# Reordering matmuls, first loads and one reduction chain in a conformer-plus-attention layer on one core

## The chip, the core and the metric

The kernel runs on one NeuronCore of a Trainium2 chip. The core has a matrix engine (PE, with a weight-load part PEld), a vector engine (DVE), a scalar engine (ACT), a GpSimd engine (POOL), a queue engine (SP), and 16 DMA engines. Each engine works through its own instruction list in order; semaphores connect the lists. The metric is the device time of one execution in microseconds (us), given as the median over runs. The time before the change is 2009.45 us, the median of 3 runs (2008.85 to 2011.46).

## The reference

One layer on 512 tokens of 2048 features, in float32:

```python
xn = rms_norm(x, attn_norm_g);  proj = xn @ w_in            # 2048 -> 5120 columns
u_val, u_gate, q, k, v = split(proj)
y_conv = silu(layer_norm(depthwise_conv31(u_val * sigmoid(u_gate))))
y_na   = neighborhood_attention(q, k, v, rpb)               # 16 heads of 64, window 8 x 16 on a 8 x 64 grid
x = x + concat(rms_norm(y_conv), rms_norm(y_na)) @ w_out    # 2048 -> 2048
xn = rms_norm(x, ffn_norm_g);  up = depthwise_conv3(xn @ w_up)   # 2048 -> 2 * 5632
x = x + (silu(gate) * val) @ w_down                         # 5632 -> 2048
return rms_norm(x, final_norm_g)
```

## The kernel before, in words

**Precision.** Every weight unit of 128 x 1024 floats is loaded by SP into a buffer `raw` (nine of them, `NR`), rounded by ACT into a high part `whi` (L125), and the remainder is taken by DVE into a low part `wlo` (L126). There are four buffers of each part (`NW`). Activations are split in the same way (`xh` and `xl`, `mah` and `mal`). A product is the sum of three matmuls: high by high, high weight by low activation, low weight by high activation. `mm3` (L138, L141, L142) issues the three for one block of 128 rows, one after the other. `weights()` hands out the units in the order of `plan`, and makes each unit three units ahead of its use (`AHEAD`).

**Input projection (up to about 515 us).** `project(n)` makes one tile of 128 output columns by 512 tokens from two units of eight blocks, so 48 matmuls of 512 columns. The first two tiles (`first_glu`) use units loaded by hand in a fixed order (`early`, `piece`, `pin`); `pin` keeps an instruction at its place in the program order on its engine, while the others are placed by a scheduler that goes by priorities. `stats1` is a generator that `tick` advances once after each unit; it loads the untransposed input in eight pieces (`xn`, L305), squares each on ACT with a running sum (L306), and makes from the sums the row factor `rstd1` by `root_steps` (the small DVE steps L224 to L234, then a matmul `st` at L237, and an ACT copy at L239). `gated` multiplies by `rstd1` (L352, L354, L356), and appends the 31 convolution steps of a tile (L363, L367) on DVE. The attention of a head pair runs in steps between the units (`sc`, `trp`, `trv` and `po` matmuls).

**Output projection (to about 708 us).** `out_half` makes 16 tiles of 512 columns from one unit each, once for the convolution half (`ma`) and once for the attention half (`mb`). In the second pass `after(d, ps)` adds the tile to the residual `x2[d]`, adds its square to `acc2` (`sum_sq`, L211 and L212), turns the tile by four PE transposes (`turned`, L594) and writes it to memory, and for each pair of tiles makes the seven operand sums of a Strassen-like scheme: scaled tiles `b` (L611), sums `t` (L616 to L621), and their high and low parts `xc` (`halves`, L586 and L587) into `comb[c]`.

**Up projection (to about 1577 us).** For each of 44 values of `f`, `up` makes seven products in the order `TURN = (3, 2, 4, 5, 1, 0, 6)`. An `xc` tile holds the high part in its first 256 columns and the low part in the other 256, so the high weight takes one matmul of 512 columns and the low weight one of 256 columns (L696): eight of the first, then eight of the second. Product 2 is made by `mm3` with three matmuls of 256 columns for each block. ACT copies and DVE adds combine the products (`copied` L706, `folded` L709 and L710). `stats2` makes `rstd2` from `acc2` during `f = 0`.

**Down projection (to the end).** `product2` makes seven products of 22 units each, into four PSUM banks. For each bank, `feed` issues three matmuls (L821 high by high, L822 with the low weight, L823 with the low activation). The last four units of the last product are done bank by bank.

Of the kernel before, what the change touches and what calls it, by code (L numbers as in the profile page):

```python
# [10 lines left out]
F32 = mybir.dt.float32  # L11
# [5 lines left out]
P = 128  # L17
D = 2048
# [32 lines left out]
NEG = -1.0e30  # L51

TURN = (3, 2, 4, 5, 1, 0, 6)
TURN2 = (3, 0, 4, 1, 2, 6, 5)
Q = D // 2 // S
TAIL = 4
# [16 lines left out]
def layer(ctx: ExitStack, tc: tile.TileContext, xT, xn, w_in, w_out, w_up, w_down, par, tab, g3, out):  # L73
# [28 lines left out]
    def pc(name, i):  # L102
        o = POFF[name] + i
        return prm[:, o:o + 1]
# [30 lines left out]
    def mm3(ps, w, wk, mh, ml, start, stop, more=False):  # L135
        hi, lo = w[:2]
        a = slice(wk * P, (wk + 1) * P)
        i = nc.tensor.matmul(ps, hi[:, a], mh, start=start, stop=False, skip_group_check=more)  # L138
        if tight:
            pin(i)  # L140
        nc.tensor.matmul(ps, hi[:, a], ml, start=False, stop=False, skip_group_check=more)  # L141
        return nc.tensor.matmul(ps, lo[:, a], mh, start=False, stop=stop, skip_group_check=more)  # L142


    steps, asteps = [], []

# [105 lines left out]
    def split_x(k):  # L252
        x1.append(t2("x"))
        i = pin(nc.sync.dma_start(x1[k], xT[k]))
        h, l = t2("xh", F32R), t2("xl", F32R)
        pin(nc.scalar.activation(h, x1[k], AF.Copy, scale=g1[:, k:k + 1]))
        pin(nc.vector.scalar_tensor_tensor(l, x1[k], g1[:, k:k + 1], h.bitcast(F32), op0=ALU.mult, op1=ALU.subtract))
        xs.append((h, l))
        return i
# [26 lines left out]
    for i in range(4):  # L286
# [7 lines left out]
    del plan[4:8]  # L294
# [20 lines left out]
    def project(n):  # L315
        ps = psm.tile([P, S], F32, tag="mm", name="pj")
        for u in range(KD // U):
            w = weights()
            for k in range(U):
                kk = u * U + k  # L320
                m = mm3(ps, w, k, xs[kk][0], xs[kk][1], kk == 0, kk == KD - 1)
            tick(m)
            if weights.at > 6 and weights.at % 2:
                sum_ahead(m)
            while late:
                late.pop()()
        return ps
# [223 lines left out]
    def out_half(m, read):  # L551
        for d in range(KD):
            w = weights()
            ps = psm.tile([P, S], F32, tag="mm", name="po2")
            for k in range(U):
                i = mm3(ps, w, k, m[k][0], m[k][1], k == 0, k == U - 1)
            tick(i)
            if d % 3 == 0:
                sum_ahead(i)
            read(d, ps)  # L560
# [38 lines left out]
    def after(d, ps):  # L599

        t = t2("oa")
        nc.vector.tensor_mul(t, ps, rb[0])
        nc.vector.tensor_add(x2[d], x2[d], t)
        sum_sq(acc2, x2[d], d == 0)
        turned(d)
        if d % 2 == 0:
            return
        b = []
        for i in (d - 1, d):
            t = t2("b")  # L610
            nc.scalar.activation(t, x2[i], AF.Copy, scale=pc("g2", i))  # L611
            b += [t[:, :H], t[:, H:]]
        b11, b12, b21, b22 = b
        t = t2("t")
        t1, t2_ = t[:, :H], t[:, H:]
        nc.vector.tensor_sub(t1, b11, b12)  # L616
        nc.vector.scalar_tensor_tensor(t2_, b22, -1.0, t1, op0=ALU.mult, op1=ALU.subtract)
        t = t2("t")
        t3, t4_ = t[:, :H], t[:, H:]
        nc.vector.tensor_sub(t3, b22, b12)  # L620
# [10 lines left out]

    def stats2():
        rstd2.append((yield from rsqrt_steps(acc2, D, "rstd2")))

    def factors(f, at):

# [48 lines left out]
    def up(f, done):  # L685

        def product(c, ps, more):
            hi, lo = wt = weights()
            if c == 2:
                for k in range(U):  # L690
                    m = comb[c][k]
                    i = mm3(ps[:, :H], wt, k, m[:, :H], m[:, H:], k == 0, k == U - 1)
            else:
                for part, n in ((hi, S), (lo, H)):
                    for k in range(U):
                        i = nc.tensor.matmul(ps[:, :n], part[:, k * P:(k + 1) * P], comb[c][k][:, :n],  # L696
                                             start=part is hi and k == 0 and not more,
                                             stop=part is lo and k == U - 1, skip_group_check=more)
                        if part is hi and k == 0 and tight:
                            pin(i)  # L700
            tick(i)
            done(TURN.index(c), i)

        def copied(to, ps):
            with shifted(-100):
                nc.scalar.activation(to, ps, AF.Copy)  # L706

        def folded(to, ps):
            nc.scalar.activation(to, ps[..., H:], AF.Copy)  # L709
            add(to, to, ps[..., :H])  # L710
# [102 lines left out]

    def product2(c, ps, more):

        def feed(w, h, i, start, stop):
            wh, wl = w
            t, d = divmod(i, Q)
            t, d = slice(t * P, (t + 1) * P), slice(d * S, (d + 1) * S)
            tl = slice(H + t.start, H + t.stop)  # L820
            nc.tensor.matmul(ps[i], h[:, t], wh[:, d], start=start and not more, stop=False, skip_group_check=more)  # L821
            nc.tensor.matmul(ps[i], h[:, t], wl[:, d], start=False, stop=False, skip_group_check=more)  # L822
            return nc.tensor.matmul(ps[i], h[:, tl], wh[:, d], start=False, stop=stop, skip_group_check=more)  # L823

        n = NK - TAIL if c == TURN2[-1] else NK
        for j in range(n):
            w, h = weights()
            for i in range(2 * Q):
                m = feed(w, h, i, j == 0, j == NK - 1)
            tick(m)  # L830
        if n < NK:
            got = [weights() for _ in range(NK - n)]
            assert not steps
            for i in range(2 * Q):
                for j, (w, h) in enumerate(got):
                    feed(w, h, i, False, j == NK - n - 1)
                yield i

    def rest(th, dh):
# [162 lines left out]
```

## Time and profile before

| | us |
|---|---|
| median of 3 runs | 2009.45 |
| the profiled execution, its own time | 2008.65 |
| its span in the trace | 2006.9 |
| PE busy | 1985.5 (99%) |
| DVE busy | 1598.5 (80%) |
| ACT busy | 1095.9 (55%) |

The span reaches from the first to the last instruction. A row of the timeline has the start, the duration, the engine, the line, the operation, the tiles, the shape and a count, and in brackets how long the engine had been idle and what ended it. Matmuls overlap in the pipeline, so the duration of one in the trace is longer than the step from one start to the next; the step is what counts here. In the view by windows each row has a stretch, then each engine's busy time and count, then the granted PE clock, the DMA share and the GB/s.

### The profile page before, as it was taken

The numbers are of one execution on the slowest core, as the hardware profiler recorded it, in microseconds if no ns is written. First come the engines' busy times: TensorE is split into PE (matmuls) and PEld (weight loads), VectorE is DVE, ScalarE is ACT, GpSimd is POOL, SyncE is SP. The second block draws the span as 40 slices with busy tenths as digits, with TensorE's granted clock in tenths as the row PEclk, the third lists the DMA queues.
The fourth block names the chain that finished last, engine by engine and source line by source line (L and its number), as shares of the span: only waits on it lengthen the run. The fifth ranks groups of instructions, "written<-read, shape, count | busy, mean of one in ns | idle before, by whom it ended". The sixth has DMA issues, their size and how long they took to land.

```text
span 2006.9 us, 28334 instructions
## 1 busy us (share of the span) xinstructions
PE 1985.5 (99%) x10525; PEld 1688.0 (84%) x10525; DVE 1598.5 (80%) x2296; ACT 1095.9 (55%) x1728; POOL 225.8 (11%) x310
## 2 busy tenths in 40 slices
PE   9999999999999999999999999999999999999998
PEld 7778888887788889888898988898898888888886
DVE  4994899488556888888888888888888898886765
ACT  6234433447534666566666666566666644554654
POOL 0111111111001111111111111111110400000000
PEclk9999999999999999999999999999999999999999
DMA  9677767766858888989999999999997877666563
GB/s 352 158 197 180 177 172 190 192 182 166 296 147 206 214 213 230 271 237 260 249 260 247 261 252 253 258 250 262 250 246 200 335 254 235 216 217 191 191 213 110
DMA packets 143115, 451.01 MB, mean 225 GB/s; under 512 B 15232, under 2 KB 23936, under 8 KB 141568
## 3 DMA queue, kind: packets, MB, share of 16 engines
q1 hardware_dynamic: 90608, 293.98, 43.0%
q0 software_dynamic: 42624, 148.92, 34.7%
q10 hardware_dynamic: 9744, 6.30, 1.0%
q8 instruction: 82, 1.34, 0.3%
q14 instruction: 57, 0.47, 0.1%
HBM read 430.27 MB, written 111.15 MB: 270 GB/s over the span
## 4 chain that ended last, share of the span: by engine, by line
PE 96%; DVE 2%; ACT 1%; DMA 1%; issue 0%; SPq 0%; DVEq 0%; ACTq 0%
PE pu L696 37%; PE pd L821 7%; PE pd L822 7%; PE pd L823 7%; PE pj L138 7%; PE pj L141 7%; PE pj L142 7%; PE po L138 3%; PE po L141 3%; PE po L142 3%; PE pu L141 2%; PE pu L142 2%; PE pu L138 2%; DVE y L367 1%; PE po L495 1%; PE sc L453 1%
## 5 line engine op out<-in xcount | busy, mean ns | idle before, releaser
L125 ACT ACTIVATE whi<-raw 128x1024 fp32r<-128x1024 f32 x572 | 605.4, 1059 | 709.7 <-PE pj L141 220.4
L126 DVE TENSOR_TENSOR wlo<-raw,whi 128x1024 fp32r<-128x1024 f32 x572 | 698.7, 1222 | 285.2 <-ACT whi L125 261.1
L696 PE MATMUL pu<-xc,whi 128*128 128x512 f32 x2112 | 529.8, 392 | 0.2 <-ACT pu L706 0.2
L696 PEld LDWEIGHTS pu<-xc,whi 128*128 128x128 f32 x2112 | 379.9, 189 | 68.8 <-issue 0.5
L696 PEld LDWEIGHTS pu<-xc,wlo 128*128 128x128 f32 x2112 | 288.1, 190 | 20.5
L696 PE MATMUL pu<-xc,wlo 128*128 128x256 f32 x2112 | 294.5, 282 | 0.0
L142 PE MATMUL pj<-xh,wlo 128*128 128x512 f32 x624 | 244.7, 392 | 7.1 <-DVE wlo L126 7.1
L138 PE MATMUL pj<-xh,whi 128*128 128x512 f32 x624 | 247.5, 399 | 0.0
L141 PE MATMUL pj<-xl,whi 128*128 128x512 f32 x624 | 245.0, 393 | 0.1
L821 PE MATMUL pd<-whi,ho 128*128 128x512 f32 x616 | 239.7, 389 | 0.5 <-DVE vl L710 0.5
L822 PE MATMUL pd<-wlo,ho 128*128 128x512 f32 x616 | 239.8, 389 | 0.0
L823 PE MATMUL pd<-whi,ho 128*128 128x512 f32 x616 | 239.5, 389 | 0.0
L367 DVE SCALAR_TENSOR_TENSOR y<-ch,prm,y 128x509 f32<-128x509 f32 (+14 forms) x240 | 170.0, 740 | 3.2
L142 PEld LDWEIGHTS pj<-xh,wlo 128*128 128x128 f32 x624 | 118.0, 189 | 33.0 <-DVE wlo L126 8.0
L138 PEld LDWEIGHTS pj<-xh,whi 128*128 128x128 f32 x624 | 118.0, 189 | 28.4 <-issue 3.7
L141 PEld LDWEIGHTS pj<-xl,whi 128*128 128x128 f32 x624 | 117.8, 189 | 24.3 <-issue 0.7
L821 PEld LDWEIGHTS pd<-whi,ho 128*128 128x128 f32 x616 | 115.7, 188 | 25.0 <-DVE vl L710 0.9
L823 PEld LDWEIGHTS pd<-whi,ho 128*128 128x128 f32 x616 | 115.7, 188 | 24.1
L822 PEld LDWEIGHTS pd<-wlo,ho 128*128 128x128 f32 x616 | 115.7, 188 | 24.1 <-DVE wlo L126 0.3
L194 POOL DMA_DIRECT2D ws<-in_w_down x88 | 79.4, 902 | 495.8 <-DMA ws<-ws 254.8
L643 POOL DMA_DIRECT2D raw<-in_w_up x88 | 86.1, 979 | 408.2 <-ACT vl L709 133.1
L138 PE MATMUL pu<-xc,whi 128*128 128x256 f32 x352 | 99.8, 284 | 1.4 <-ACT xc L586 1.4
(185 smaller groups left out, 2526.0 us busy)
## 6 DMA issues: line engine op xcount, KB each, us to landing
raw<-in_w_up SPq DMA_DIRECT2D x220, 512.0 KB, 7.2
ws<-in_w_down POOLq DMA_DIRECT2D x132, 512.0 KB, 7.4
raw<-in_w_up POOLq DMA_DIRECT2D x88, 512.0 KB, 8.5
raw<-ws SPq DMA_DIRECT2D x88, 512.0 KB, 3.4
raw<-in_w_in SPq DMA_DIRECT2D x78, 512.0 KB, 4.8
raw<-in_w_down SPq DMA_DIRECT2D x66, 512.0 KB, 4.2
ws<-ws POOLq DMA_DIRECT2D x44, 512.0 KB, 7.5
raw<-in_w_out SPq DMA_DIRECT2D x32, 512.0 KB, 4.9
```

The costliest lines, as they stand in the source:

```text
L125: i = nc.scalar.activation(hi[:, :n], raw[:, :n], AF.Copy)
L126: j = nc.vector.tensor_sub(lo[:, :n], raw[:, :n], hi[:, :n].bitcast(F32))
L138: i = nc.tensor.matmul(ps, hi[:, a], mh, start=start, stop=False, skip_group_check=more)
L141: nc.tensor.matmul(ps, hi[:, a], ml, start=False, stop=False, skip_group_check=more)
L142: return nc.tensor.matmul(ps, lo[:, a], mh, start=False, stop=stop, skip_group_check=more)
L194: nc.gpsimd.dma_start(wsum[c][k], w_down[k, {1: A21, 2: A11, 4: A11, 6: A12}[c]], accum_op=ALU.add, max_dma_last_dim=ROW)
L367: nc.vector.scalar_tensor_tensor(y[:, a:b], h[:, a + j - PAD:b + j - PAD], prm[:, o + j:o + j + 1], y[:, a:b], op0=ALU.mult, op1=ALU.add)
L643: nc.gpsimd.dma_start(a[c], w_up[f, q2], accum_op=ALU.add)
L696: i = nc.tensor.matmul(ps[:, :n], part[:, k * P:(k + 1) * P], comb[c][k][:, :n], start=part is hi and k == 0 and not more, stop=part is lo ...
L821: nc.tensor.matmul(ps[i], h[:, t], wh[:, d], start=start and not more, stop=False, skip_group_check=more)
L822: nc.tensor.matmul(ps[i], h[:, t], wl[:, d], start=False, stop=False, skip_group_check=more)
L823: return nc.tensor.matmul(ps[i], h[:, tl], wh[:, d], start=False, stop=stop, skip_group_check=more)
```

## The change

There are five edits, and the arithmetic is the same sums in another order.

1. Low parts last. A new function `group` replaces `mm3` in `project` and `out_half`: for a unit of eight blocks it issues the sixteen matmuls with the high weight, and then the eight with the low weight. In `product2`, `feed` goes by kind: high by high for all banks, then the low activation, then the low weight. `first_glu` and product 2 of `up` keep `mm3`.
2. First loads. The two units of the third projected tile (`NC_ + 1`) and the eight pieces of `xn` with their squares move from the plan and from `stats1` into the pinned opening, in front of the load of the parameters `prm`. `stats1` is left with waiting three ticks, the reduction and the root.
3. The last pair's sums. In `after`, the scaled tile `b` is made as soon as its `x2[d]` is there, the seven operands of a pair are made and split in the order in which `up` uses them, and `sum_sq` comes behind them. `turned` comes one or two tiles later, and for the last tile after the statistics in `stats2`.
4. Order in `up`. The products in `FIRST = (3, 5, 0)` issue the 512-column matmuls first; the products 4, 1 and 6 issue the 256-column matmuls with the low weight first.
5. For `f = 0` product 3 goes block by block, 512 and 256 columns in turn.

```diff
+FIRST = (3, 5, 0)
...
+    def group(ps, ws, ms, first, last):
+
+        for k, ((hi, _, wk), (mh, ml)) in enumerate(zip(ws, ms)):
+            hi = hi[:, wk * P:(wk + 1) * P]
+            nc.tensor.matmul(ps, hi, mh, start=first and k == 0, stop=False)
+            nc.tensor.matmul(ps, hi, ml, start=False, stop=False)
+        for k, ((_, lo, wk), (mh, _)) in enumerate(zip(ws, ms)):
+            i = nc.tensor.matmul(ps, lo[:, wk * P:(wk + 1) * P], mh, start=False, stop=last and k == len(ws) - 1)
+        return i
...
     for k in range(U, KD):
-        last = split_x(k)
+        split_x(k)
+    squares = sm.tile([P, S // P, 2], F32, tag="ss", name="ss")
+    for u in range(2):
+        raw, i = raw_unit(w_in[NC_ + 1, :, u * U * P:(u + 1) * U * P], U * P)
+        pin(i)
+        for t in range(2 * u, 2 * u + 2):
+            for i in range(2):
+                x = t4([P, D // 2], "xn")
+                pin(nc.sync.dma_start(x, xn[t * P:(t + 1) * P, i * D // 2:(i + 1) * D // 2]))
+                if t == 2 * u and i == 0:
+                    w = parts(raw, U * P)
+                    pin(w[2])
+                    pin(w[3])
+                    early.append(w[:2])
+                pin(nc.scalar.activation(x, x, AF.Square, accum_out=squares[:, t, i:i + 1]))
     last = pin(nc.sync.dma_start(prm, par))
...
     def stats1():
-        part = sm.tile([P, S // P, 2], F32, tag="ss", name="ss")
-        for t in range(S // P):
-            for i in range(2):
-                x = t4([P, D // 2], "xn")
-                nc.sync.dma_start(x, xn[t * P:(t + 1) * P, i * D // 2:(i + 1) * D // 2])
-                nc.scalar.activation(x, x, AF.Square, accum_out=part[:, t, i:i + 1])
-            if t < S // P - 1:
-                yield
+        for _ in range(3):
+            yield
         sums = sm.tile([P, S // P], F32, tag="s1", name="s1")
-        nc.vector.tensor_reduce(sums, part, axis=AX.X, op=ALU.add)
+        nc.vector.tensor_reduce(sums, squares, axis=AX.X, op=ALU.add)
...
-            for k in range(U):
-                kk = u * U + k
-                m = mm3(ps, w, k, xs[kk][0], xs[kk][1], kk == 0, kk == KD - 1)
+            m = group(ps, [(*w, k) for k in range(U)], xs[u * U:(u + 1) * U], u == 0, u == KD // U - 1)
...
-        sum_sq(acc2, x2[d], d == 0)
-        turned(d)
+        t = t2("b")
+        nc.scalar.activation(t, x2[d], AF.Copy, scale=pc("g2", d))
+        bs[d % 2] = t[:, :H], t[:, H:]
         if d % 2 == 0:
             return
...
+        halves(b11, 3)
+        nc.vector.tensor_sub(t3, b22, b12)
+        halves(t3, 2)
         nc.vector.tensor_sub(t1, b11, b12)
         nc.vector.scalar_tensor_tensor(t2_, b22, -1.0, t1, op0=ALU.mult, op1=ALU.subtract)
+        halves(t2_, 4)
+        halves(b21, 5)
+        halves(t1, 1)
         nc.vector.scalar_tensor_tensor(t4_, t2_, -1.0, b21, op0=ALU.mult, op1=ALU.subtract)
-        for c in TURN:
-            halves((t4_, t1, t3, b11, t2_, b21, b22)[c], c)
+        halves(t4_, 0)
+        halves(b22, 6)
+        for i in (d - 1, d):
+            sum_sq(acc2, x2[i], i == 0)
+        for i in (d - 2, d - 1):
+            if i >= 0:
+                turned(i)
...
         rstd2.append((yield from rsqrt_steps(acc2, D, "rstd2")))
+        turned(KD - 1)
...
-                for part, n in ((hi, S), (lo, H)):
-                    for k in range(U):
+                turns = [(part, n, k) for part, n in ((lo, H), (hi, S))[::-1 if c in FIRST else 1]
+                         for k in range(U)]
+                if f == 0 and c == 3:
+                    turns.sort(key=lambda a: a[2])
...
+        def feed(got, banks, start, stop):
+
+            for kind in range(3):
+                for i in banks:
+                    t, d = divmod(i, Q)
+                    d = slice(d * S, (d + 1) * S)
+                    for j, ((wh, wl), h) in enumerate(got):
+                        o = H if kind == 1 else 0
+                        w = wl if kind == 2 else wh
+                        m = nc.tensor.matmul(ps[i], h[:, o + t * P:o + (t + 1) * P], w[:, d],
...
```

More of the change, by code (lines that the diff above doesn't have):

```diff
@@ L283, in layer @@
     for k in range(U, KD):
-        last = split_x(k)
+        split_x(k)
[13 more added lines that the diff above has]
+                pin(nc.scalar.activation(x, x, AF.Square, accum_out=squares[:, t, i:i + 1]))
     last = pin(nc.sync.dma_start(prm, par))
-    for i in range(4):
+    for i in range(len(early)):
         plan.append(lambda i=i: early[i])
@@ L293, in layer @@
                 plan.append(lambda n=n, u=u: unit(w_in[n, :, u * U * P:(u + 1) * U * P], U * P))
-    del plan[4:8]
+    del plan[6:12]
     for half in range(2):
@@ L554, in out_half @@
             ps = psm.tile([P, S], F32, tag="mm", name="po2")
-            for k in range(U):
-                i = mm3(ps, w, k, m[k][0], m[k][1], k == 0, k == U - 1)
+            i = group(ps, [(*w, k) for k in range(U)], m, True, True)
             tick(i)
@@ L693, in product @@
             else:
-                for part, n in ((hi, S), (lo, H)):
[L695 to L700, printed above, removed]
+                turns = [(part, n, k) for part, n in ((lo, H), (hi, S))[::-1 if c in FIRST else 1]
+                         for k in range(U)]
+                if f == 0 and c == 3:
+                    turns.sort(key=lambda a: a[2])
+                for j, (part, n, k) in enumerate(turns):
+                    i = nc.tensor.matmul(ps[:, :n], part[:, k * P:(k + 1) * P], comb[c][k][:, :n],
+                                         start=j == 0 and not more, stop=j == 2 * U - 1, skip_group_check=more)
+                    if j == 0 and tight:
+                        pin(i)
             tick(i)
@@ L814, in product2 @@
     def product2(c, ps, more):
[L816 to L823, printed above, removed]
+        def feed(got, banks, start, stop):
[7 more added lines that the diff above has]
+                        m = nc.tensor.matmul(ps[i], h[:, o + t * P:o + (t + 1) * P], w[:, d],
+                                             start=start and not more and kind == 0 and j == 0,
+                                             stop=stop and kind == 2 and j == len(got) - 1, skip_group_check=more)
+            return m
         n = NK - TAIL if c == TURN2[-1] else NK
         for j in range(n):
[L827 to L830, printed above, removed]
+            tick(feed([weights()], range(2 * Q), j == 0, j == NK - 1))
         if n < NK:
@@ L834, in product2 @@
             for i in range(2 * Q):
-                for j, (w, h) in enumerate(got):
-                    feed(w, h, i, False, j == NK - n - 1)
+                feed(got, [i], False, True)
                 yield i
```

15 lines of the change are left out of this document (4 added, 11 removed).

## The prediction

> **What bounds the kernel now.** I read the page first (share of each engine and the chain that ended last), then PE's waits, then the timelines of PE, DVE and ACT around each place where PE stands, and last the steps from start to start of PE's matmuls where it does not stand.
>
> ```profile
> span 2006.9 us, 28334 instructions
> ...
> PE 1985.5 (99%) x10525; PEld 1688.0 (84%) x10525; DVE 1598.5 (80%) x2296; ACT 1095.9 (55%) x1728; POOL 225.8 (11%) x310
> ...
> PE 96%; DVE 2%; ACT 1%; DMA 1%; issue 0%; SPq 0%; DVEq 0%; ACTq 0%
> ...
> PE pj L142 <- DVE wlo L126: 7.1, 2, 3.8
> PE pu L138 <- ACT xc L586: 1.4, 1, 1.4
> ```
>
> PE is 99% busy and carries 96% of the chain, and the change keeps every matmul of the sums. So there are two things to win: the few stretches where PE stands or runs at a lower clock, and steps between matmuls that are longer than they need be. The waits name the largest: two waits for a low part, 7.1 us together. Each is followed by a stretch at half clock, as the windows show (the clock is the number behind POOL's):
>
> ```profile
> 58.40:61.80 3.40, 3.40 (x9) 2.63 (x8) 3.40 (x5) 0.00 (x0) 0.00 (x0) 0.50 0.60 180
> ...
> 106.40:110.00 3.60, 3.60 (x9) 2.87 (x10) 3.60 (x5) 0.00 (x0) 0.00 (x0) 0.56 0.64 195
> ```
>
> Half clock costs 3.40 x 0.50 = 1.7 us and 3.60 x 0.44 = 1.6 us.
>
> **Part 1, the opening (edits 1 and 2).** PE, DVE and ACT around the two waits:
>
> ```profile
> 30.53 0.39 PE L138 MATMUL pj<-xh,whi 128*128 128x512 f32 x1
> ...
> 45.49 1.02 PE L237 MATMUL st<-dg,ones 128*128 128x512 f32 x2
> ...
> 53.41 0.39 PE L141 MATMUL pj<-xl,whi 128*128 128x512 f32 x1
> ...
> 57.16 0.50 PE L142 MATMUL pj<-xh,wlo 128*128 128x512 f32 x1 [3.35 <-DVE wlo L126]
> ...
> 101.99 0.39 PE L138 MATMUL pj<-xh,whi 128*128 128x512 f32 x1
> ...
> 106.38 0.80 PE L142 MATMUL pj<-xh,wlo 128*128 128x512 f32 x1 [3.78 <-DVE wlo L126]
> ```
>
> ```profile
> 40.33 0.88 DVE L234 TENSOR_SCALAR dg<-ident,rsy 128x128 f32<-128x128 f32 x4
> ...
> 47.18 0.69 DVE L352 TENSOR_TENSOR gate<-pj,rstd 128x512 f32<-128x512 f32 x1 [4.84 <-ACT rstd L239]
> ...
> 55.89 2.35 DVE L126 TENSOR_TENSOR wlo<-raw,whi 128x1024 fp32r<-128x1024 f32 x2
> ...
> 102.55 0.69 DVE L423 TENSOR_TENSOR k<-pj,rstd 128x512 f32<-128x512 f32 x1
> ...
> 105.10 2.36 DVE L126 TENSOR_TENSOR wlo<-raw,whi 128x1024 fp32r<-128x1024 f32 x2
> ```
>
> ```profile
> 46.54 0.60 ACT L239 ACTIVATE rstd<-st 128x512 f32<-128x512 f32 x1 [6.38 <-PE st L237]
> ...
> 51.71 3.88 ACT L125 ACTIVATE whi<-raw 128x1024 fp32r<-128x1024 f32 x4
> ```
>
> The step of a 512-column matmul comes from the down projection, where nothing interrupts:
>
> ```profile
> 1986.04 0.39 PE L821 MATMUL pd<-whi,ho 128*128 128x512 f32 x1
> ...
> 1988.08 0.61 PE L821 MATMUL pd<-whi,ho 128*128 128x512 f32 x2
> ...
> 1988.61 0.50 PE L822 MATMUL pd<-wlo,ho 128*128 128x512 f32 x1
> ```
>
> 1986.04 to 1988.08 is nine steps, 0.2267 us each; a unit of 24 takes 5.44 us, its sixteen high-weight matmuls 3.63 us. The first wait costs 57.16 - 53.41 - 0.23 = 3.5 us and 1.7 us of clock, the second 106.38 - 102.21 (one step after 101.99) - 0.23 = 3.9 us and 1.6 us: 10.7 us.
>
> Do they go? DVE's queue is late because rstd is: dg is ready at 41.2, but the matmul that uses it stands behind 18 matmuls of the next unit, at 45.49. In the changed program that matmul stands right behind the last pinned unit: 30.53 + 2 x 5.44 = 41.41. The eight squares come without prm and without one weight unit ahead of the last of them, so dg is ready by 41.2 at the latest; what could be late is prm, which now lands behind them, and DVE's reading of it stands ahead of the reduction. I take no wait. Then rstd's first reader on DVE, 1.69 us behind the matmul's start (45.49 to 47.18), runs at 43.1 instead of 47.18, and ACT's next high parts stand 4.1 us earlier than 51.71. The low part of the first wait was started 8.7 us behind that reader; the same work plus some convolution steps puts it near 52, done by 53.5. Its unit starts at 41.41 + 0.9 + 2 x 5.44 = 53.2, and now first needs it 3.63 us later. This wait goes, with 3 us to spare.
>
> The second: the unit that started at 101.99 now starts at 53.2 + 8 x 5.44 = 96.7 and needs its low part at 100.35. DVE's queue from rstd to that part has two convolution steps fewer than the 57.9 us between 47.18 and 105.10 held, so DVE would be there at 43.1 + 57.9 - 1.3 + 1.2 = 100.9 at the latest. A floor comes from PE: the reader of k stands ahead of it, can't run before 96.7 + 0.25, and the part starts 2.55 us (102.55 to 105.10) behind it and takes 1.2: 100.75. So 0.4 to 1 us of waiting stays, too short for what the clock did after 3.4 us; I take 0.45. Gain **10.3 us**, bounds 9.3 and 10.7.
>
> What hides the moved loads: they go on SP in nearly the order they had; the next weight unit is now behind prm, and is needed at 42.3.
>
> **Part 2, the order of widths in up (edits 4 and 5).**
>
> ```profile
> 853.35 0.28 PE L138 MATMUL pu<-xc,whi 128*128 128x256 f32 x1
> ...
> 856.23 2.00 PE L696 MATMUL pu<-xc,whi 128*128 128x512 f32 x8
> ...
> 738.55 16.76 PE pu L696 x96
> ...
> 1543.79 16.76 PE pu L696 x96
> ```
>
> Product 2 is 24 matmuls of 256 columns between 853.35 and 856.23: 0.120 us each. One f takes (1543.79 - 738.55)/41 = 19.640 us, so each of its six other products takes (19.640 - 2.88)/6 = 2.793 us. Eight steps of 0.2267 and eight of 0.120 are 2.774. So a change from 256 columns to 512 and back costs 0.020 us on balance: the weight load of a 256-column step lags, and the first wide matmuls pay it. Now there are six such pairs for each f; in the new order 3 | 2 | 4, 4 | 5, 5 | 1, 1 | 0, 0 | 6, 6 | 3 there are three. 44 x 3 x 0.020 = **2.6 us**, if the cost goes by the change and not by the number of narrow matmuls in a run; if it doubles with the run's length, nothing is won. I take 2.6, since the cost shown is one per product whether 8 or 32 narrow ones stand before it. [...]
>
> Low first in products 4, 1 and 6: the low part is needed 1.8 us sooner, and ACT's reuse of that high buffer 0.95 us later. Parts are made three units ahead, 3 x 2.79 = 8.4 us; the two conversions take some 1.1 and 1.2. Cost 0.
>
> **Part 3, the turns and the last pair (edit 3).** A turn that follows an addition just made, and one that does not:
>
> ```profile
> 694.25 0.39 PE L142 MATMUL po<-mbh,wlo 128*128 128x512 f32 x1
> ...
> 695.15 0.40 PE L141 MATMUL po<-mbl,whi 128*128 128x512 f32 x1
> ...
> 697.00 0.40 PE L138 MATMUL po<-mbh,whi 128*128 128x512 f32 x1
> ...
> 698.08 0.39 PE L142 MATMUL po<-mbh,wlo 128*128 128x512 f32 x1
> ...
> 707.63 0.85 PE L683 MATMUL pu<-xc 128*128 128x512 f32 x3
> ...
> 717.49 2.11 PE L696 MATMUL pu<-xc,whi 128*128 128x512 f32 x8 [0.17 <-ACT pu L706]
> ```
>
> Both stretches hold two wide matmuls and four transposes: 0.90 and 1.08 us. In the timeline eight of the sixteen turns are of the longer kind, each behind the first matmul of a tile, and all are late enough now: 8 x 0.17 = **1.3 us** (bounds 0 and 1.5).
>
> From 707.63 to 717.49 PE does 11 wide matmuls (2.49), 32 narrow (3.84), one turn (0.45) and the eight statistics matmuls (0.9): 7.7 us, so 2.2 are lost, 1.4 of them in the wait on xc. Now product 3's operand of the last pair needs only the tile before the last, whose `b` is already made; but on ACT its high part stands behind the last `b`. With PE doing product 3 block by block and five matmuls of product 2 first, about 3 us, the two arrive together. I take 0.3 us left: **1.9 us** (bounds 0 and 2.2). The statistics matmuls come 17 matmuls later, and acc2 with them; cover is about half a microsecond.
>
> **Part 4, down (edit 1, and edit 4's price).**
>
> ```profile
> 1576.29 1.11 PE L696 MATMUL pu<-xc,wlo 128*128 128x256 f32 x8
> 1577.24 0.40 PE L821 MATMUL pd<-whi,ho 128*128 128x512 f32 x1
> ...
> 1580.63 0.50 PE L821 MATMUL pd<-whi,ho 128*128 128x512 f32 x1 [0.48 <-DVE vl L710]
> ...
> 1576.53 1.06 ACT L125 ACTIVATE whi<-raw 128x1024 fp32r<-128x1024 f32 x1 [1.73 <-PE pu L696]
> ```
>
> Here the change adds a wait. ACT's high part at 1576.53 waits for product 6 to leave its high buffer (its wide matmuls end at 1576.29); behind it on ACT stand the copies of the last f, behind these DVE's additions, and PE waits for those at 1580.63, after twelve matmuls into the other two banks. With product 6 low first, the buffer is left at 1577.24: 0.95 us later, for ACT, DVE and PE alike. **+0.95 us** (bounds 0 and 1).
>
> At the end, the last low part came 0.1 us late (1988.61), and the matmuls around it lost 0.35 us; low weights last hide that: **0.35 us**. Going round four banks costs nothing: L823 to L821 changes bank today in the nine steps above.
>
> **Sum.** -10.3 - 2.6 - 1.3 - 1.9 + 0.95 - 0.35 = -15.5 us on the profiled execution's 2008.65 (span 2006.9, 1.75 around it): 1993.2. That execution lies 0.8 under the median of 2009.45; I say 1993.5.
>
> **Rivals.**
>
> A. PE waits at the moved statistics matmul. If dg came 4 us later than 41.4 (prm behind the squares, DVE's reading of it ahead of the reduction), PE would stand 4 us and run some 1.7 us at half clock, 5.5 in all: 1998.7. For it: prm's new place, and that the loads leave no gap here. Against: there is less ahead of the squares than before, when dg was there at 41.2.
>
> B. The order of widths is free or goes by the run's length: term 2 is zero, 1995.8. [...]
>
> C. Slower: ACT holds PSUM copies behind a high part whose buffer is left later, as in part 4, but in all 132 low-first products.
>
> ```profile
> 859.24 0.58 ACT L706 ACTIVATE pu<-pu 128x512 f32<-128x512 f32 x1
> ...
> 861.82 2.00 PE L696 MATMUL pu<-xc,whi 128*128 128x512 f32 x8
> ```
>
> The shift is 0.95 us, 125 us if all of it reached PE; from 15.5/132 = 0.12 us per product the kernel is slower than before. Against: the copy of product 4's bank is done at 859.82 and first needed by product 1 at 861.82, 2.0 us of room. If it decides, some 0.2 us per product: 2020.
>
> **Chances.** The sum 0.76, A 0.10, B 0.07, C 0.07, of which 0.02 end within 0.2% (4 us, about what a measurement of this kernel can tell from no change). Faster 0.93, same 0.02, slower 0.05. Low end: every gain at its better bound and no price, 10.7 + 2.6 + 1.5 + 2.2 + 0.35 = 17.4, with the profiled execution's own time 1991.2, and I go to 1990.8. High end: A and the poorer bounds of part 3, 1999.5.
>
> **What would show it.** No wait of pj on wlo over 1 us, and a clock of 1.0 from 20 us to the last slice; the statistics matmul near 41.4; 19.58 us per f; product 4 of f = 0 starting about 2 us sooner after the three preparing matmuls; a wait of about 1.4 us at the start of down. I am wrong if PE waits at L248 (the moved matmul), if an f still takes 19.64, or if new waits of PE on ACT appear in up.

## The result and the profile after

The changed kernel takes **1992.5 us** (median of 5 runs, 1991.97 to 1993.17) against 2009.45 before (2008.85 to 2011.46, 5 runs beside it): a ratio of 0.991, with a 95% interval of 0.9897 to 0.9924. The forecast was 1993.5. The profiled execution took 1993.17 with a span of 1991.4; that of before took 2008.65 with 2006.9, so both differ by the 15.5 us that the prediction summed. The exactness is luck: the medians differ by 16.95 us, the profiled execution after is the longest of its five, and several errors of the terms cancel.

From the page of the changed kernel, its span, its busy times and the shares of the chain:

```profile
span 1991.4 us, 28519 instructions
...
PE 1976.7 (99%) x10525; PEld 1685.7 (85%) x10525; DVE 1593.1 (80%) x2296; ACT 1100.4 (55%) x1728; POOL 225.4 (11%) x310
...
PE 96%; DVE 2%; DMA 1%; ACT 0%; issue 0%; SPq 0%; DVEq 0%
```

PE bounds it as before, and is busy 8.8 us less for the same 10525 matmuls (1985.5 before): the half clock and part of the longer steps are gone. From the waits of PE (us in total, times, longest):

```profile
PE pj L139 <- ACT xh L267: 1.6, 2, 0.9
PE pd L848 <- DVE vl L733: 1.4, 1, 1.4
...
PE pj L153 <- DVE wlo L127: 0.8, 1, 0.8
```

Of the 7.1 us in two waits for a low part one of 0.8 us is left, and the wait that the change adds at the start of down is there with 1.4 us. The first row is for the first activations, in the first 14 us; it differs from run to run (0.2 us in u7, which has the same opening). The windows of the changed kernel show no half clock around the wait for the low part (the number behind POOL's is the granted clock):

```profile
50.00:100.00 50.00, 50.00 (x222) 41.42 (x221) 48.29 (x69) 11.22 (x12) 6.56 (x9) 1.00 0.69 177
100.00:108.00 8.00, 7.19 (x33) 5.61 (x32) 8.00 (x9) 1.55 (x2) 0.51 (x1) 1.00 0.56 168
```

The opening in PE's timeline and in DVE's:

```profile
41.85 1.02 PE L248 MATMUL st<-dg,ones 128*128 128x512 f32 x2
...
100.55 0.39 PE L151 MATMUL pj<-xl,whi 128*128 128x512 f32 x1
101.74 1.43 PE L153 MATMUL pj<-xh,wlo 128*128 128x512 f32 x5 [0.81 <-DVE wlo L127]
```

```profile
97.92 0.68 DVE L440 TENSOR_TENSOR k<-pj,rstd 128x512 f32<-128x512 f32 x1
98.52 2.03 DVE L384 SCALAR_TENSOR_TENSOR y<-ch,prm,y 128x505 f32<-128x505 f32 x3
100.47 2.35 DVE L127 TENSOR_TENSOR wlo<-raw,whi 128x1024 fp32r<-128x1024 f32 x2
```

The statistics matmul stands at 41.85 without a wait (41.41 forecast). The second low part is begun 2.55 us behind the reader of `k`, and PE comes to it 101.74 - 100.55 - 0.23 = 0.97 us too early.

Where the time went, by the starts of the same matmuls in both traces (us):

| stretch | before | after | difference |
|---|---|---|---|
| start to the first attention transpose (`trv`) | 123.87 | 114.57 | -9.30 |
| to the matmul of the mean's statistics | 332.61 | 331.82 | -0.79 |
| to the attention half of the output projection | 155.63 | 155.66 | +0.03 |
| to the three preparing matmuls of up | 95.52 | 93.73 | -1.79 |
| to the first matmul of down | 869.61 | 865.26 | -4.35 |
| the first unit of down | 6.24 | 7.14 | +0.90 |
| to the last matmul | 413.56 | 413.63 | +0.07 |
| to the end | 9.85 | 9.57 | -0.28 |

Kernels with the same opening lie up to 1.6 us apart in the first row (112.98 to 114.61); the difference is there by the statistics matmul, which stands between 40.23 and 41.87. So the experiments are compared by stretches and not by their ends alone.

### The profile page after: what moved, and what is told of

Its sections match the earlier page's. It is cut to its first block, busy times and chain, and to the rows that moved or that the text cites. A ratio compares the mean times of both kernels' runs of the same rounds, so it can differ in the third digit from the quotient of the medians.

```text
span 1991.4 us, 28519 instructions
## 1 busy us (share of the span) xinstructions
PE 1976.7 (99%) x10525; PEld 1685.7 (85%) x10525; DVE 1593.1 (80%) x2296; ACT 1100.4 (55%) x1728; POOL 225.4 (11%) x310
## 4 chain that ended last, share of the span: by engine, by line
PE 96%; DVE 2%; DMA 1%; ACT 0%; issue 0%; SPq 0%; DVEq 0%
PE pu L720 37%; PE pd L848 21%; PE pj L150 7%; PE pj L153 7%; PE pj L151 7%; PE po L150 3%; PE po L151 3%; PE po L153 3%; PE pu L143 2%; PE pu L142 2%; PE pu L139 2%; DVE y L384 1%; PE sc L470 1%; PE po L512 1%; PE trp L498 1%; DMA raw<-in_w_in 0%
## 5 line engine op out<-in xcount | busy, mean ns | idle before, releaser
L720 PE MATMUL pu<-xc,whi 128*128 128x512 f32 x2112 | 505.5, 391 | 0.1
L720 PEld LDWEIGHTS pu<-xc,whi 128*128 128x128 f32 x2112 | 388.0, 188 | 75.3 <-DVE xc L603 0.3
L848 PE MATMUL pd<-whi,ho 128*128 128x512 f32 x1232 | 305.1, 389 | 1.4 <-DVE vl L733 1.4
L720 PEld LDWEIGHTS pu<-xc,wlo 128*128 128x128 f32 x2112 | 274.4, 191 | 10.3
L720 PE MATMUL pu<-xc,wlo 128*128 128x256 f32 x2112 | 282.3, 283 | 0.0
L384 DVE SCALAR_TENSOR_TENSOR y<-ch,prm,y 128x510 f32<-128x510 f32 (+14 forms) x240 | 169.8, 739 | 3.1
L848 PE MATMUL pd<-wlo,ho 128*128 128x512 f32 x616 | 165.0, 389 | 0.0
L153 PE MATMUL pj<-xh,wlo 128*128 128x512 f32 x608 | 150.4, 389 | 0.8 <-DVE wlo L127 0.8
L729 ACT ACTIVATE pu<-pu 128x512 f32<-128x512 f32 x132 | 76.5, 580 | 121.4 <-PE pu L720 121.2
L139 PE MATMUL pu<-xc,whi 128*128 128x256 f32 x352 | 99.6, 283 | 0.0
L142 PE MATMUL pu<-xc,whi 128*128 128x256 f32 x352 | 99.6, 283 | 0.0
```

Source lines behind the costliest of these rows:

```text
L153: i = nc.tensor.matmul(ps, lo[:, wk * P:(wk + 1) * P], mh, start=False, stop=last and k == len(ws) - 1)
L384: nc.vector.scalar_tensor_tensor(y[:, a:b], h[:, a + j - PAD:b + j - PAD], prm[:, o + j:o + j + 1], y[:, a:b], op0=ALU.mult, op1=ALU.add)
L848: m = nc.tensor.matmul(ps[i], h[:, o + t * P:o + (t + 1) * P], w[:, d], start=start and not more and kind == 0 and j == 0, stop=stop and k ...
```

## The experiments

Each is the changed kernel with one part undone or changed (u4 undoes two edits). All compute the same sums. The changed kernel was run again beside two of them.

**after_again**, no edit.

> The changed kernel once more, beside the two others: 1992.5 within 1 us.

1992.97 us (1992.17 to 1993.45), and every row of the table above within 0.15 us. Differences between medians below about half a microsecond are not read; the stretches of the traces are.

### The opening: which half of it pays

**u1_opening**, edit 2 undone:

```diff
-    squares = sm.tile([P, S // P, 2], F32, tag="ss", name="ss")
-    for u in range(2):
-        raw, i = raw_unit(w_in[NC_ + 1, :, u * U * P:(u + 1) * U * P], U * P)
...
     def stats1():
-        for _ in range(3):
-            yield
+        part = sm.tile([P, S // P, 2], F32, tag="ss", name="ss")
+        for t in range(S // P):
+            for i in range(2):
+                x = t4([P, D // 2], "xn")
+                nc.sync.dma_start(x, xn[t * P:(t + 1) * P, i * D // 2:(i + 1) * D // 2])
...
```

> The opening is put back (edit 2 undone: the third tile's units in the plan, the untransposed input loaded and squared between the units), the low parts stay last. Theory: both halves of the opening's gain are needed. The statistics matmul is back near 45.5 us and the first reader of rstd near 47.2. Low parts last forgive 3.6 us, so of the first wait about 0.3 us is left, but the second low part is ready near 106.3 and needed near 102.2: a wait of about 4 us and some 1.6 us of lower clock, against 1.08 us of waiting now. Sum +5 us: 1997.5 (1996 to 1999), first attention transpose about 5 us later than the 114.57 of the changed kernel. Rival, low parts last are enough: both waits under 1 us, 1992.5 to 1993.5.

1998.85 us (1998.53 to 1999.25); the first `trv` at 119.93, 5.36 us later than in the changed kernel, and no other stretch differs by more than 0.1. PE's timeline and a window around its second wait:

```profile
101.26 0.39 PE L151 MATMUL pj<-xl,whi 128*128 128x512 f32 x1
105.73 3.42 PE L153 MATMUL pj<-xh,wlo 128*128 128x512 f32 x8 [4.08 <-DVE wlo L127]
```

```profile
98.00:114.00 16.00, 11.92 (x47) 9.40 (x46) 16.00 (x22) 2.12 (x2) 0.54 (x2) 0.89 0.60 164
```

105.73 - 101.26 - 0.23 is 4.24 us of waiting, and the eight matmuls behind it take 0.41 us a step instead of 0.227, until 108.99. Low parts last do not replace the earlier statistics: the theory holds, and the rival falls.

**u2_low**, edit 1 undone in both projections and in down:

```diff
-            m = group(ps, [(*w, k) for k in range(U)], xs[u * U:(u + 1) * U], u == 0, u == KD // U - 1)
+            for k in range(U):
+                kk = u * U + k
+                m = mm3(ps, w, k, xs[kk][0], xs[kk][1], kk == 0, kk == KD - 1)
...
```

> The low parts are put back (edit 1 undone in the two projections and in down: the three matmuls of a block side by side), the new opening stays. Theory: rstd stays near 43 us, the first low part is ready at 53.5 and needed at 53.4, so no first wait; the second is ready at 101.7 as now but needed at 97.1 instead of 100.5: a wait of about 4.4 us and some 1.6 us of lower clock against 1.08 us now, +4.9 us, and some 0.3 us at the end of down: 1997.7 (1996 to 1999). Rival, the earlier statistics are enough: 1992.5 to 1993.5.

1996.53 us (1995.25 to 1996.87). The profiled execution, the shortest of the four, is 2.1 us longer in its span than that of the changed kernel: 0.98 up to the first `trv`, 0.80 up to the mean's statistics, 0.3 net behind (0.44 less up to the preparing matmuls, 0.70 more from there to down). The median lies in the range that was expected, but in this execution the opening loses 1 us and not the 4.9 of the theory. PE's timeline and DVE's:

```profile
96.88 0.39 PE L142 MATMUL pj<-xl,whi 128*128 128x512 f32 x1
99.50 0.50 PE L143 MATMUL pj<-xh,wlo 128*128 128x512 f32 x1 [2.24 <-DVE wlo L127]
```

```profile
96.98 0.68 DVE L442 TENSOR_TENSOR k<-pj,rstd 128x512 f32<-128x512 f32 x1
97.58 0.73 DVE L386 SCALAR_TENSOR_TENSOR y<-ch,prm,y 128x505 f32<-128x505 f32 x1
98.23 2.35 DVE L127 TENSOR_TENSOR wlo<-raw,whi 128x1024 fp32r<-128x1024 f32 x2
```

The wait is 2.4 us and not 4.4, because DVE's list is another one: one convolution step stands between the reader of `k` and the low part, where the changed kernel has three, and the part is begun at 98.23 instead of 100.47. In this execution the clock did not drop behind it. The other three took 1.2 to 1.6 us more than the profiled one; where they lost that is not shown. With the earlier statistics in place, undoing low parts last costs 2.1 us by the two traces and 4.0 by the medians. Up to the first `trv`, by the traces, they are worth 0.98 us with the earlier statistics and 3.94 without them (before against u1). The two edits overlap: each saves most where the other is missing.

### The order of widths

**u3_widths**:

```diff
-FIRST = (3, 5, 0)
+FIRST = (3, 4, 5, 1, 0, 6)
```

> All six products of up with 512 columns first (edit 4 undone, edit 5 kept). Theory: a change from 256 to 512 columns costs 0.020 us, six of them for each f instead of three: an f takes 19.64 us again instead of 19.58, +2.6 us over 44, and the start of down loses 0.95 us less: +1.65, 1994.1. Rival, the order of widths is free: f stays at 19.58 and only the start of down moves, 1991.6.

**n3_fours**:

```diff
+                if f:
+                    turns = [(p, n, k) for ks in (range(4), range(4, U)) for p, n in ((hi, S), (lo, H)) for k in ks]
```

> From the second f on, every product but product 2 goes four matmuls of 512 columns, four of 256, four of 512, four of 256: twelve changes from narrow to wide for each f instead of three, with the same matmuls. Theory, the cost goes by the change: 19.58 + 9 x 0.020 = 19.76 us for each f, 43 x 0.18 = +7.7 us: 2000 (1998 to 2001). Rival, the cost goes by the number of narrow matmuls in a run: their number is what it was, so an f takes no more than 19.64, 1992.5 to 1995. Rival, free: 1992.5.

1994.66 us (1994.61 to 1994.8) and 1998.43 (1997.65 to 1998.65). The chain that ended last names product rows of 96 matmuls once for each f; the same two of them, 41 f apart, in the changed kernel, in u3 and in n3:

```profile
724.91 16.70 PE pu L720 x96
...
1527.69 16.70 PE pu L720 x96
```

```profile
724.67 16.76 PE pu L720 x96
...
1529.91 16.76 PE pu L720 x96
```

```profile
724.47 16.84 PE pu L722 x96
...
1532.99 16.84 PE pu L722 x96
```

An f takes 802.78/41 = 19.580 us with three changes from narrow to wide, 805.24/41 = 19.640 with six, and 808.52/41 = 19.720 with twelve. The matmuls are the same, so the cost does go by the change, and an order of widths is not free. It is 0.020 us for each of the three changes between the first two; without any change an f would then take 19.520, and n3's twelve cost 0.200 us, 0.017 each, eleven of them behind a run of four narrow matmuls and all ahead of a run of four wide ones. So a short run costs somewhat less. The starts of the matmuls show where the time goes: in the changed kernel the first five wide steps behind a change take 0.233, 0.236, 0.228, 0.233 and 0.231 us (means over forty f), and the others 0.227; in n3 a wide run ends before the fifth. In n3 the stretch of up is 5.99 us longer, 43 times 0.139, below the 7.7 expected; the median lies in the range expected. u3 also gives the 0.9 us at the start of down back, as expected.

### The turns and the last pair

**u4_pair**, edits 3 and 5 undone, and **u5_turns**, the turns alone:

```diff
+        turned(d)
         t = t2("b")
         nc.scalar.activation(t, x2[d], AF.Copy, scale=pc("g2", d))
...
-        for i in (d - 2, d - 1):
-            if i >= 0:
-                turned(i)
...
-        turned(KD - 1)
```

> Edits 3 and 5 undone: turns, square sums and the last pair's operands as before, product 3 of the first f with its wide matmuls first. Theory: the turns cost 1.3 to 1.8 us again (the three preparing matmuls come that much later), and between them and the first matmul of down the last pair's 1.8 us come back: +3.5, 1996 (1995 to 1997), with the wait of PE on xc at 1.4 us again. Rival, the gain at the end of the output projection came with the low parts last and not with the turns: +1.8, 1994.3.

> Only the turns go back to their old place, right behind the addition of their tile; the order of the last pair's sums stays. Theory: eight turns wait some 0.17 to 0.2 us each, the preparing matmuls start 1.3 to 1.8 us later, nothing changes behind them: 1994.1. Rival, the turns were free and the 1.8 us in the output projection have another cause (low parts last): 1992.5.

1998.71 us (1997.6 to 2000.16) and 1998.63 (1998.21 to 1998.7): each costs some 6 us, far more than either theory had. That is the price in the changed kernel, with its low parts last; over the kernel before, the two stretches had gained 1.79 + 4.35 less 2.64 of widths, 3.5 us. The cut shows u5; u4 undoes with it what u6 and u7 below undo singly. u4 is 0.40 us later at the preparing matmuls of up, and loses 6.52 from there to the first matmul of down. Its wait for the last pair's high part is back with 1.8 us (1.4 was expected), and a stretch at half clock follows:

```profile
PE pu L139 <- ACT xc L602: 1.8, 1, 1.8
```

```profile
705.00:712.30 7.30, 7.11 (x30) 6.82 (x31) 5.23 (x15) 4.47 (x10) 0.00 (x0) 0.54 0.49 94
```

In the trace the half clock lasts from 705.52 to 712.35, with PE busy throughout, so it costs 6.83 x 0.50 = 3.4 us; with two waits of 0.85 and 1.85 us that is 6.1 of the 6.52. Two of u4's four executions are 2.2 us shorter than the profiled one; what they did not lose is not shown. In u5 the clock stays at full. It is 1.79 us later at the preparing matmuls, and the fourteen turns ahead of them take 8.07 us instead of 0.44 each, 1.9 more; another 4.11 us lie between there and down, at the last pair. Waits of PE in u5:

```profile
PE trx L610 <- DVE x L619: 1.5, 5, 0.8
...
PE pu L717 <- ACT pu L726: 1.0, 1, 1.0
...
PE pu L701 <- DVE oa L618: 0.9, 1, 0.9
```

The first and the last lead to DVE's two steps for the addition of a tile (L618, then L619), at the last pair to those of the tile before the last. In the changed kernel, and then in u5, the row that begins the operands of the pair before, and the row that begins that addition:

```profile
687.28 0.42 DVE L629 TENSOR_TENSOR t<-b 128x256 f32<-128x256 f32 x1
...
692.86 0.68 DVE L618 TENSOR_TENSOR oa<-po,rna 128x512 f32<-128x512 f32 x1
```

```profile
693.93 0.42 DVE L630 TENSOR_TENSOR t<-b 128x256 f32<-128x256 f32 x1
...
700.37 0.68 DVE L618 TENSOR_TENSOR oa<-po,rna 128x512 f32<-128x512 f32 x1
```

The addition is 7.5 us later in u5. In both lists the operands of the pair before stand ahead of it; in u5 they begin 6.65 us later. To find which part does that, the three parts were undone singly.

**u6_blocks**, edit 5 alone:

```diff
-                if f == 0 and c == 3:
-                    turns.sort(key=lambda a: a[2])
```

> Only edit 5 undone: product 3 of the first f issues its 512-column matmuls first again instead of block by block. Theory: the low weights of product 3 can then only follow its eighth block, so PE reaches the last pair's operand after seven wide matmuls and what it finds of product 2; the operand is there at the same time as now, so the 0.3 us of waiting grows by at most 1 us: 1992.5 to 1993.5, nothing else moves. Rival, edit 5 carries the last pair's 1.8 us: 1994.3.

**u7_sums**, the order of the sums alone:

```diff
-        t = t2("b")
-        nc.scalar.activation(t, x2[d], AF.Copy, scale=pc("g2", d))
-        bs[d % 2] = t[:, :H], t[:, H:]
+        sum_sq(acc2, x2[d], d == 0)
         if d % 2 == 0:
             return
...
+        for c in TURN:
+            halves((t4_, t1, t3, b11, t2_, b21, b22)[c], c)
```

> Only the order of the sums in edit 3 undone: squares right behind the addition, both scaled tiles and all seven operands made at the end of a pair in the old order; the turns stay late and edit 5 stays. Theory from the two runs before: what those lost beyond 1.8 us each came from DVE's list, in which the operands of the earlier pair stand ahead of the last two tiles' additions (4 and 7 us later than in the changed kernel). If the sums' order alone does that, the wait at the last pair is 3 us or more and the kernel some 4 to 6 us slower: 1996.5 to 1998.5. If it needs the turns in their old place, only the wait on xc of 1.4 us comes back: 1994.

1993.03 us (1992.28 to 1993.24) and 1993.02 (1992.85 to 1993.29): neither makes a difference that the medians show (by the traces u7 is 0.27 us shorter in the stretch to down and 0.87 longer behind the last matmul; why is not shown). In u7 the wait at the last pair is no longer than in the changed kernel, by the row in front of the last pair's operand and the one that reads it:

```profile
700.09 0.28 PE L142 MATMUL pu<-xc,whi 128*128 128x256 f32 x1
700.47 0.50 PE L717 MATMUL pu<-xc,whi 128*128 128x512 f32 x1
```

0.38 us with one step of 0.12, so 0.26 lost; the changed kernel loses 0.21 at the same place. The operand is later with the old sums: it is read 5.17 us behind the first preparing matmul, and 4.04 in the changed kernel. But PE has fourteen matmuls of product 2 to do before it instead of five. Both branches of that expectation are wrong: neither 3 us nor 1.4 us of waiting comes with the old sums, as long as the turns are late. Edit 5 and the order of the sums were not undone together with the turns late, so it is not shown that the gain would stay without both.

**u8_last_turns**, only the first fourteen turns back:

```diff
+        if d < KD - 2:
+            turned(d)
         t = t2("b")
...
-        for i in (d - 2, d - 1):
-            if i >= 0:
-                turned(i)
+        if d == KD - 1:
+            turned(d - 1)
```

> The first fourteen turns back in their old place, the last two stay late; sums and edit 5 stay. Theory: what the run with all turns back lost beyond its turns (3.8 us at the last pair) comes from the last two turns alone; then the last pair keeps what it has, and fourteen turns cost 0.14 us more each, as in that run: +2.0, 1995 (1994 to 1995.5). Rival, turns in the old place anywhere put DVE's additions of the last two tiles behind the operands of the earlier pair: 1998 and more, as with all turns back.

1998.46 us (1997.89 to 1999.3): the rival. So the last two turns alone are not what matters. ACT's timeline of u8 at the pair before the last, and DVE's:

```profile
690.70 0.60 ACT L612 ACTIVATE xt<-trx 128x512 f32<-128x512 f32 x1 [0.52 <-PE trx L610]
691.20 0.71 ACT L623 ACTIVATE b<-x,prm 128x512 f32<-128x512 f32 x1
```

```profile
688.94 0.68 DVE L619 TENSOR_TENSOR x<-x,oa 128x512 f32<-128x512 f32 x1
...
692.74 0.42 DVE L631 TENSOR_TENSOR t<-b 128x256 f32<-128x256 f32 x1
...
699.20 0.68 DVE L618 TENSOR_TENSOR oa<-po,rna 128x512 f32<-128x512 f32 x1
```

The tile is added by 689.6. Its scaled form `b` stands on ACT behind the copy of the turned tile, which waits for PE's turn; `b` begins at 691.20, the pair's operands on DVE at 692.74, and the next tile's addition only behind them, at 699.20. In the changed kernel the rows for its addition and its `b` are these:

```profile
685.15 0.69 DVE L619 TENSOR_TENSOR x<-x,oa 128x512 f32<-128x512 f32 x1
```

```profile
685.87 0.73 ACT L621 ACTIVATE b<-x,prm 128x512 f32<-128x512 f32 x1 [2.17 <-DVE x L619]
```

There `b` begins 0.7 us behind the start of its addition, in u8 2.3. So a turn close to its addition couples PE, ACT and DVE, and lateness is handed from tile to tile. That the copy on ACT is the link is read from the timelines; no run moves the copy alone. Why the scheduler lists DVE's work in this order then is not shown.

### The start of down

**n1_last_wide**:

```diff
-                turns = [(part, n, k) for part, n in ((lo, H), (hi, S))[::-1 if c in FIRST else 1]
+                turns = [(part, n, k) for part, n in ((lo, H), (hi, S))[::-1 if c in FIRST or (f, c) == (NF - 1, 6) else 1]
```

> One edit on the changed kernel: product 6 of the last f issues its 512-column matmuls first. Theory: the high part that stands ahead of the last copies on ACT gets its buffer 0.95 us sooner, the wait of PE at the start of down falls from 1.4 us to about 0.5: -0.9, 1991.6. Rival, DVE's own queue sets that wait: 1992.5.

**n2_order**:

```diff
     def unit2(c, k):
-        return unit(wsum[c][k] if c in wsum else w_down[k, {0: A22, 3: A11, 5: A12}[c]], U * P)
+        w = parts(raw_unit(wsum[c][k] if c in wsum else w_down[k, {0: A22, 3: A11, 5: A12}[c]], U * P)[0], U * P)
+        if (c, k) == (TURN2[0], order2[AHEAD]):
+            pin(w[2])
+        return w[:2]
```

> One edit on the changed kernel: ACT makes the high part of the fourth unit of down behind the last f's copies instead of ahead of them. Theory: the copies run as soon as their banks are done, the wait at the start of down goes wholly: -1.5, 1991.0. Rival, DVE's additions or the high part now made late take its place (a wait of PE on whi near 1577 us): 1992.5 or more.

1991.94 us (1991.59 to 1992.36) and **1990.93** (1990.68 to 1991.02), beside 1992.97 of the changed kernel in the same set. ACT and PE at the start of down, first in the changed kernel:

```profile
1561.24 1.06 ACT L126 ACTIVATE whi<-raw 128x1024 fp32r<-128x1024 f32 x1 [2.65 <-PE pu L720]
1562.21 0.64 ACT L732 ACTIVATE g<-pu 128x256 f32<-128x256 f32 x2
1562.74 0.66 ACT L732 ACTIVATE vl<-pu 128x256 f32<-128x256 f32 x2
```

```profile
1561.04 1.07 PE L848 MATMUL pd<-whi,ho 128*128 128x512 f32 x4
...
1565.33 1.20 PE L848 MATMUL pd<-whi,ho 128*128 128x512 f32 x4 [1.41 <-DVE vl L733]
```

and then in n2:

```profile
1560.64 0.38 ACT L735 ACTIVATE g<-pu 128x256 f32<-128x256 f32 x1 [2.37 <-PE pu L723]
1560.92 0.66 ACT L735 ACTIVATE vl<-pu 128x256 f32<-128x256 f32 x2
...
1567.47 4.84 ACT L126 ACTIVATE whi<-raw 128x1024 fp32r<-128x1024 f32 x5
```

```profile
1560.44 1.07 PE L851 MATMUL pd<-whi,ho 128*128 128x512 f32 x4
...
1565.88 1.98 PE L851 MATMUL pd<-whi,ho 128*128 128x512 f32 x8
```

The first unit of down takes 7.14 us in the changed kernel, 6.23 in n1 and 5.44 in n2, which is the length of a unit without any wait: the cause is the order on ACT, wholly. No wait on the later high part appears. n2 is the best of all versions here, 2.0 us under the changed kernel, of which 1.70 lie in this unit.

## Why the prediction was right, and where its steps were not

**Opening.** The mechanism held: the statistics matmul moved without a wait, the first wait went, the second shrank to 0.97 us, and the clock stays at 1.00 from 4.67 us to 1984.40. The residual was mis-sized: 0.45 was taken, 0.97 and 0.11 behind it were lost, the upper end of its 0.4 to 1. The stretch gained 9.30 and not 10.3: 0.6 of the difference is this, and 0.4 that the statistics matmul stands at 41.85 and not 41.41, behind the waits for the first activations. The floor from PE assumed that the reader of `k` runs as soon as its tile is done (96.95); it ran at 97.92, because DVE had convolution steps in front of it. The 2.55 us from there to the low part were right.

**A gain that was not foreseen.** PE's wait in front of the mean's statistics is gone, 0.79 us with what hung on it. The row of before, in PE's timeline:

```profile
456.48 1.10 PE L382 MATMUL st<-acc,ones 128*128 128x512 f32 x2 [0.45 <-DVE s L461]
```

It is back in u2 and absent in u1, so edit 1 removes it.

**Widths.** Right in place and size: 19.58 us for an f was forecast and measured, and n3 shows that it goes by the change. Rival B is out. The Trainium skill, page "TensorE: Matmul & The Clock Gate", section "Back-to-back issue gap", gives a formula by column count for an isolated matmul, and says that in a stream of weight loads and matmuls both set the spacing. By column count alone the three f times would be equal, and they are not; that the weight loads make the difference is not shown here.

**Turns.** 1.3 was forecast. Fifteen turns take 6.55 us instead of 8.04, so 1.5, and 0.3 more in the matmuls beside them.

**Last pair.** 1.9 was forecast. Of the 4.35 us in that stretch 44 times 0.060 are the widths, so 1.7 is the last pair's: the size was right, but the step behind it was wrong. The prediction let the operand arrive with PE because `b` and the sums stand in the order of use and product 3 goes block by block; u6 and u7 show that neither, undone by itself, costs anything here. The part without which the gain goes (u5, u8) is the late turns, which had been costed only for their 0.17 us of waiting; that they carry it alone is not shown. The prediction looked at each turn on PE's list, and not at the copy of the turned tile that it issues on ACT ahead of `b`.

**Down.** +0.95 was forecast, 0.90 measured, with n1 (-0.91) and n2 as proof of its cause. The tail gained 0.28 less 0.07 and not 0.35. u2, with the old order in down, loses 0.11 of the 0.28 again and wins back the 0.07, 0.04 net. So it is not shown that low weights last bring the tail's gain.

**The others.** Rival A: the moved matmul does not wait. Rival C: no wait of PE on ACT appears in up, and an f keeps its 19.580 us, so the copies' room of 2.0 us covers the later high parts. The sum came out by luck: 1.0 us too much in the opening stands against 0.8 unforeseen and 0.5 at the turns. The high end of the range does not follow from its own words: A with the poorer bounds of part 3 is 1998.7 + 1.3 + 1.9 = 2001.9, not 1999.5.

## What to carry to other kernels

A step that is moved carries what it issues on every engine: here one PE transpose brings an ACT copy, and moving the two away from their addition was worth more than the transpose's own wait. Undoing one part of a change under a scheduler measures that part and the new lists of all engines, so read the stretch and the lists before you call the difference the part's price; parts can overlap (u1 and u2), or cost nothing when undone singly though the sum seemed to need them (u6 and u7). A wait of a microsecond or two at a seam between stages can be one in-order list with an early instruction that blocks on a late buffer: look at what stands behind it.

## What the runs showed of the hardware

Matmuls of 256 columns step at 0.120 us, more than half of the 0.2267 of those of 512, and a change from narrow to wide costs 0.017 to 0.020 us on top, in the first wide steps behind it. Both are steps in the traces; that the weight load sets them is only argued.

The lower clock does not follow from one wait's length alone. It came behind waits of 3.35, 3.78 and 4.08 us, and behind one of 1.85 (u4), and not behind one of 2.24 (u2). u5 and u8 have the same two waits of 0.87 and 0.79 us within 2.4 us of each other, and behind them one window shows full clock and the other half; first u5, then u8:

```profile
702.40:706.00 3.60, 3.60 (x29) 3.40 (x29) 1.51 (x3) 2.75 (x5) 0.36 (x1) 1.00 0.85 168
```

```profile
702.20:705.40 3.20, 3.20 (x17) 3.20 (x16) 2.32 (x7) 1.45 (x3) 0.00 (x0) 0.50 0.97 152
```

The traces show what differs. Within each run the clock changes only at times that lie whole multiples of 3.41 us apart: it is half from 58.39 to 61.80 and from 106.17 to 109.59 before, from 105.16 to 108.57 in u1, from 705.52 to 712.35 in u4 and from 702.05 to 705.47 in u8. If these times are carried on as a grid, both waits of u8 lie in one stretch, 698.64 to 702.05, in which PE stands 1.66 us; in u5 a border at 700.97 cuts them into 0.73 and 0.93, and in u2 a border at 98.22 cuts the 2.24 into 0.96 and 1.28. From the first full clock to the last matmul, half clock followed every stretch of the grid in which PE stood 1.66 us or more (1.66, 1.85, 2.18, and twice the whole 3.41) and none with 1.41 or less (the wait at the start of down, whole in one stretch in five runs). Stretches that hold the last matmul kept full clock with up to 1.93 us, so the border is not exact, and why u4's half clock lasted two stretches is not shown.

PE lost 3.41 x 0.50 = 1.7 us of work in u8, though the stretch to down is only 0.42 us longer than u5's. Short waits that stand close together are worth removing for this reason too.
